# Hybrid decoder layer on one core: buffer sets of heads, inverses by rows over 128 partitions, later steps on transferred tiles, moved convolution pairs

## Chip, core and metric

The kernel runs on one NeuronCore of a Trainium2 chip (trn2). The time is the device time of one execution in microseconds (us), the median over runs; lower is better.

## What is computed

One layer with two groups of heads that run side by side, for 2048 tokens of width 1024, float32. One RMSNorm and one projection to 8208 columns feed both; a second projection brings 2048 columns back to 1024, a residual is added, and a last RMSNorm closes it.

```python
proj = rmsnorm(x, norm_in_w) @ w_in                        # 2048 x 1024 @ 1024 x 8208
qkv  = silu(causal_depthwise_conv(qkv, conv_qkv_w))        # 8 heads x 128, 4 taps
q, k = l2norm(q) * 128**-0.5, l2norm(k); beta = sigmoid(b_g)
g    = -exp(A_log) * softplus(a_g + dt_bias)               # decay of each head and token
# per head, chunk by chunk (WY form): A = strict(k beta k^T * decay), T = (I + A)^-1
u, w = T @ (v beta), T @ (k beta exp(g))
v_new = u - w S;  o = (q exp(g)) S + causal(q k^T * decay) v_new
S = S exp(g_last) + (k exp(g_last - g))^T v_new            # state 128 x 128, carried on
o   = rmsnorm(o, gdn_norm_w) * silu(z_g)
y_c = gate_b * (conv3(gate_c * h_c) + conv_b) * silu(z_c)  # 8 groups x 128 channels
out = rmsnorm(x + concat(o, y_c) @ w_out, final_norm_w)
```

## The kernel before

**Halves and pairs.** The tokens are done in two halves of 1024. In each half the projection is made as 32 *pairs* of 128 columns: `kq` (keys and queries of a head), `vz` (its values and output gate), `ca` and `cb` (the convolution group). `quad` makes a pair with seven products of 512 columns on TensorE (Strassen's form, float16 in two parts), 84 matmuls of 128x128 by 128x512 for each pair, from the tiles `xop` and the weights `g` (first half) or `gr` (second half, loaded from DRAM). The weights of the first half are loaded as `raw`, squared, scaled and split by ScalarE (ACT), VectorE (DVE) and GpSimd (POOL) while the first half runs; they are also written to DRAM (`wc`). Pair results stand in six tiles `t4` (`c1`, `c2`, `vacc`, ...), and a pair starts only when enough of them are free.

**Heads.** `gdn` runs for 16 heads (8 in each half; `idx` is the head's number over both). The steps: the convolved keys and queries go to two tiles `kq` (one for each block of 512 tokens); products of keys with keys and queries times the decay go to two tiles `NA`; the 32x32 blocks on the diagonal go by DMA to DRAM (`nd`) and back as `nb`, one block on each of 32 partitions; `invert` inverts them on POOL in place (60 TENSOR_TENSOR instructions); the inverse goes by DMA to DRAM (`wd`) and into `Wt`, when the head before has finished with it; DVE transposes to `Vt` and small matmuls (`Q`) put together the 128x128 inverse; then eight chunks of the recurrence follow (`ps_r`, `r`, `u`, `S_all`, with the output in the one PSUM bank `ps_o`). `gdn_post` copies the output from `ps_o` to `oc`, norms it, multiplies by the gate (`zb`, read back from DRAM) and stores it (`mixd`).

**Buffers.** `kq` and `NA` are rings of four tiles. The same rings serve before at the start (`x2`, the tokens of the first half) and in `later_x`, which prepares the second half's tokens in 16 steps (`x2` and `o16`), each step ending in a DMA to `x1d`. Head 0 begins after the first half's tokens; head 1's keys wait for the end of `later_x` (the mark `x1d`); each later head's keys wait for the recurrence of the head two before. The first thing that `gdn_post` of head 0 does is to wait for `x1d`.

**Order.** The instructions of each engine stand in one fixed order. A planner in the kernel (`Clock`, `do`) issues them while it follows its own estimate of each engine's time: a step is put into its engine's queue when the estimate says that its inputs are there, with a lead for each engine (`LEAD`; 0 for DVE), and `either` picks POOL or DVE for an addition. A number in `do(..., lead=-4.0)` puts the step that much later than its inputs. At run time an engine that waits for one instruction's input holds up all behind it.

Of the kernel before, what the change touches and what calls it, by code (L numbers as in the profile page):

```python
# [23 lines left out]
DRAIN, SEM = 0.2, 0.06  # L24
SAFE = -4.0
LEAD = {"PE": -0.4, "ACT": 0.0, "DVE": 0.0, "POOL": 0.0, "SP": -2.0}
# [200 lines left out]
def hybrid_layer_kernel(ctx, tc, x, norm_in_w, w_in, conv_qkv_w, A_log, dt_bias, gdn_norm_w,  # L227
# [65 lines left out]
    def mark(*key):  # L293
        done.add(key)
        marks[0] += 1
# [65 lines left out]
    def acq(kind):  # L361
        while not slots[kind]:
            yield None
        return bank(kind)
# [41 lines left out]
    for n in range(2 * CB):  # L406
        x2 = hd.tile([P, NC * P], F32, tag=("kq", "NA")[n // CB], name="x2", bufs=4)
        xt0.append(x2[:, 0:D])
# [17 lines left out]
    for half in range(2):  # L426
        convs = [(f, half, g) for g in range(G) for f in ("ca", "cb")]
        for i in range(H):
            pair("kq", half, i)
            if i == 0:  # L430
                plan.append(("gates", half, 0, None))
            n = ((4, 2, 2, 2, 2, 2, 1, 1), (2, 1, 2, 1, 2, 1, 2, 2))[half][i]
            for c in convs[:n]:
                pair(*c)
            convs = convs[n:]
            pair("vz", half, i)
        for c in convs:
            pair(*c)
# [152 lines left out]
    def first_x():  # L591
# [14 lines left out]
        def block0():  # L606
            for k in range(KD):
                pt = yield from acq("t")
                yield from trans(pt, k, 0)
                o = xop[X11 if k < KT else X21]  # L610
                yield from do(ACT.activation, kept(k), pt, AF.Copy, scale=sx_of(k))
                rel(pt)
                yield from split16(o[:, k % KT], kept(k))
                mark("x", X11 if k < KT else X21, k % KT)

        def block1():
            for i in range(CB, 2 * CB):
                yield from norm_tile(xt0[i], junk[:, i % 2])
            for kt in range(KT):
# [5 lines left out]
                yield from do(ACT.activation, f22, pt, AF.Copy, scale=sx_of(kt + KT))  # L625
                rel(pt)
                pt = yield from acq("t")
                yield from trans(pt, kt, 1)
# [20 lines left out]
    def later_x():  # L649
        yield from need(("x0",), ("rows",))  # L650
        xs = [hd.tile([P, NC * P], F32, tag="kq", name="x2", bufs=4) for _ in range(2)]
        ovs = []
        for _ in range(2):
            o16 = hd.tile([P, NC * P], F32, tag="NA", name="o16", bufs=4)
            ovs.append(o16.bitcast(F16)[:, 0:14 * QW].rearrange("p (o s w) -> p o s w", o=7, s=2))
# [364 lines left out]


    def taps(half, t, raw, accs, p, k, key):
        yield from need(key)
# [66 lines left out]
    def sumsq(acc, src):  # L1090
        junk = sm.tile([P, P], BF16, tag="junk", name="junk")
        yield from do(ACT.activation, junk, src, AF.Square, accum_out=acc)

    def gdn(half, h, st):
# [40 lines left out]
        for b in range(2):  # L1135
# [53 lines left out]
        for b in range(2):  # L1189
            yield from do(DVE.tensor_tensor, kqs[b][:, :, 1, :], qe[:, b * CB:(b + 1) * CB], kqs[b][:, :, 1, :],  # L1190
                          op=ALU.mult)

# [18 lines left out]
        for a, q0 in ((0, 0), (2, 0), (1, 32)):  # L1211
            r0 = a * 32
            yield from do(DVE.transpose, V[r0:r0 + 32, :, q0:q0 + 32], W[r0:r0 + 32, :, r0:r0 + 32])
        Q = hd.tile([P, NC, 64], F32, tag="Q", name="Q")
# [70 lines left out]
    def gdn_post(half, h, b, po, qss):  # L1285
        idx = half * H + h
        nq = CB * 4
        sl = slice(b * nq, (b + 1) * nq)
        if idx == 0:
            yield from need(("x1d",))  # L1290
        if idx or b:
# [9 lines left out]
        yield from do(DVE.transpose, on, osq)  # L1301
        op = sm.tile([P, nq], F32, tag="op", name="op")
# [12 lines left out]
        yield from do(DVE.tensor_tensor, ocv, ocv, osq, op=ALU.mult)  # L1315
        yield from do(DVE.scalar_tensor_tensor, zb, oc, gnw, zb, op0=ALU.mult, op1=ALU.mult)
        t0 = half * NC + b * CB
# [4 lines left out]
    def invert(nb, W, idx):  # L1322
        npart = 4 * NC
        tmp = hd.tile([npart, 16 * 16], F32, tag="nbt", name="nbt")
# [6 lines left out]
        yield from do(POOL.memset, nb.rearrange("p r x -> p (r x)")[:, 0:1024:33], -1.0)  # L1331
# [113 lines left out]
    def split_mix():  # L1445
        for t in range(NT):
# [13 lines left out]
            if t < 4:  # L1460
                yield from need(("rec", 2 * H - 2 + t // 2, 1))
            else:
                yield from need(("mixfree", t - 4))
            for h in range(2):
                m = hd.tile([P, 2, KM // 2 * P], F16, tag=("kq", "NA")[t % 2], name="mm", bufs=4)
                mr = mraw.pop((t, h))
# [156 lines left out]
```

## Time and profile before

| | |
|---|---|
| median of 3 runs | 2098.22 us (2096.51 to 2103.34) |
| profiled execution | 2094.53 us, span 2092.8 us |
| PE (TensorE) busy | 1914.5 us, 91% of the span |
| DVE busy | 1390.3 us, 66% |
| ACT busy | 960.5 us, 46% |
| POOL busy | 1003.3 us, 48% |
| TensorE clock granted | 0.967 of 2.4 GHz, mean |

The profile is one execution. An engine's busy time is the time in which at least one of its instructions runs; the matmuls' ends are modelled. Idle time of an engine matters only where others wait for it. All instructions that the planner issues carry one line number, so groups are read by their tiles: `NA<-ps_t,cj,E` writes `NA` from `ps_t`, `cj` and `E`.

### The profile page before, as it was taken

The page shows a single profiled execution, that of the slowest core. Times are in us where ns is not written, and L with a number is a line of the kernel's source. Part 1 is how long each engine was busy: PE and PEld are TensorE (multiplying, and loading weights), DVE is VectorE, ACT ScalarE, POOL GpSimd, SP SyncE. Part 2 cuts the span into 40 slices and gives each one's busy share as a digit, 9 for nine tenths or more (in the row PEclk, how much of TensorE's full clock was granted, in tenths as well). Part 3 has the DMA queues.
Part 4 walks back from the last instruction along what each step waited for, and adds up shares of the span by engine and source line. Part 5 has one row for each costly group of instructions (what it writes and reads, how often), then busy time and mean ns, then how long its engine had stood idle before and what let it go on. Part 6 is the DMA issues. An engine that isn't in the chain of part 4 may idle for free.

```text
span 2092.8 us, 29911 instructions
## 1 busy us (share of the span) xinstructions
PE 1914.5 (91%) x10832; PEld 1041.8 (50%) x10832; DVE 1390.3 (66%) x2547; ACT 960.5 (46%) x1879; POOL 1003.3 (48%) x1238
## 2 busy tenths in 40 slices
PE   3798996798888989888999999999999999999998
PEld 2343443345444545444566565565665664444443
DVE  5788777988686889895757667766766553532311
ACT  6565656555444555653545435344344232532300
POOL 3227521678383858597372774746755721100000
PEclk9899998899898999999999999999999999999999
DMA  5466676455776675447365456564344348433110
GB/s 148 101 175 155 175 184 165 111 135 143 96 148 107 150 151 155 126 131 292 124 187 160 126 191 195 192 189 145 119 130 125 103 134 312 151 99 113 61 51 30
DMA packets 231194, 302.66 MB, mean 145 GB/s; under 512 B 48381, under 2 KB 161414, under 8 KB 230150
## 3 DMA queue, kind: packets, MB, share of 16 engines
q1 hardware_dynamic: 231046, 300.75, 52.0%
q8 instruction: 85, 1.39, 0.3%
q14 instruction: 63, 0.52, 0.1%
HBM read 188.36 MB, written 112.33 MB: 144 GB/s over the span
## 4 chain that ended last, share of the span: by engine, by line
PE 53%; POOL 6%; DMA 4%; DVE 3%; issue 2%; ACT 1%; SPq 0%; DVEq 0%; POOLq 0%; ACTq 0%
PE ps_d L202 43%; PE ps_t L202 6%; POOL nb L202 3%; PE ps_r L202 3%; POOL nbt L202 2%; PE ps_o L202 2%; DMA raw<-in_w_in_dram 1%; DVE kq L202 1%; DVE g L202 1%; DMA wd<-nb 1%; DMA zb<-zd 1%; DMA wc<-g 1%; DVE c L202 0%; DMA mr<-mixd 0%; POOL raw L202 0%
## 5 line engine op out<-in xcount | busy, mean ns | idle before, releaser
L202 PE MATMUL ps_d<-xop,g 128*128 128x512 f16 x2688 | 659.4, 393 | 57.0 <-ACT c L202 26.0
L202 PE MATMUL ps_d<-xop,gr 128*128 128x512 f16 x2688 | 645.2, 379 | 2.6 <-DMA xop<-x1d 2.6
L202 PEld LDWEIGHTS <-g 128*128 128x128 f16 x2688 | 266.1, 101 | 349.1 <-issue 86.8
L202 PEld LDWEIGHTS <-gr 128*128 128x128 f16 x2688 | 261.2, 99 | 241.2 <-issue 3.2
L202 POOL TENSOR_TENSOR nbt<-nb 32x30 f32<-32x30 f32 (+14 forms) x480 | 317.8, 662 | 84.1 <-DMA nb<-nd 49.3
L202 POOL TENSOR_TENSOR nb<-nb,nbt 32x30 f32<-32x30 f32 (+14 forms) x480 | 331.5, 691 | 35.8
L202 ACT ACTIVATE c<-ps_d 128x512 f32<-128x512 f32 x320 | 189.5, 593 | 325.4 <-PE ps_d L202 306.3
L202 PE MATMUL ps_d<-wo,mm 128*128 128x512 f16 x1536 | 333.9, 380 | 4.0 <-ACT mm L202 3.6
L202 PEld LDWEIGHTS <-mm 128*128 128x128 f16 x1536 | 149.5, 98 | 186.7 <-ACT mm L202 5.5
L202 POOL TENSOR_TENSOR oss<-oss,nhalf_pow 128x16 f32<-128x16 f32 x32 | 99.6, 3114 | 155.1 <-DVE oss L202 155.1
L202 DVE SCALAR_TENSOR_TENSOR kq<-c,wq,kq 128x512 f32<-128x512 f32 x192 | 166.7, 872 | 4.6
L202 POOL TENSOR_TENSOR p<-p,nhalf_pow 128x2 f32<-128x2 f32 (+1 forms) x51 | 40.9, 801 | 199.3 <-DVE p L202 168.3
L202 DVE SCALAR_TENSOR_TENSOR res<-ps_d,msc,res 128x512 f32<-128x512 f32 x32 | 22.6, 746 | 168.9 <-PE ps_d L202 168.9
L202 POOL TENSOR_TENSOR c<-c,c 128x512 f32<-128x512 f32 (+1 forms) x33 | 57.3, 1738 | 159.8 <-ACT c L202 114.8
L202 DVE SCALAR_TENSOR_TENSOR g<-raw,wsc,g 128x1024 f16<-128x1024 f32 (+1 forms) x96 | 116.5, 1221 | 11.5 <-ACT g L202 11.2
L202 ACT ACTIVATE g<-raw,wsc 128x1024 f16<-128x1024 f32 (+1 forms) x96 | 95.8, 1001 | 59.4 <-PE ps_d L202 24.2
L202 POOL TENSOR_TENSOR stat<-stat,nhalf_pow 128x1 f32<-128x1 f32 x16 | 9.7, 604 | 234.0 <-DVE stat L202 234.0
L202 DVE TENSOR_TENSOR c<-ps_d,c 128x512 f32<-128x512 f32 x128 | 87.3, 682 | 42.5 <-PE ps_d L202 41.2
L202 ACT ACTIVATE mm<-mr,msc 128x1024 f16<-128x1024 f32 x32 | 36.0, 1145 | 158.5 <-PE ps_d L202 125.1
L202 ACT ACTIVATE u<-ps_r 128x128 f32<-128x128 f32 x128 | 35.2, 275 | 147.2 <-PE ps_r L202 144.5
L202 POOL TENSOR_TENSOR raw<-raw 128x512 f32<-128x512 f32 x31 | 41.8, 1349 | 119.6 <-DVE st L202 74.4
L202 DVE TENSOR_TENSOR c<-c,c 128x512 f32<-128x512 f32 (+1 forms) x63 | 58.3, 926 | 52.1 <-ACT c L202 49.8
(226 smaller groups left out, 2794.7 us busy)
## 6 DMA issues: line engine op xcount, KB each, us to landing
gr<-wc SPq DMA_DIRECT2D x96, 512.0 KB, 3.9
raw<-in_w_in_dram SPq DMA_DIRECT2D x64, 512.0 KB, 11.2
wc<-g SPq DMA_DIRECT2D x64, 512.0 KB, 9.1
wc<-g SPq DMA_DIRECT2D x96, 256.0 KB, 4.5
wor<-in_w_out_dram SPq DMA_DIRECT2D x32, 512.0 KB, 5.5
mr<-mixd SPq DMA_DIRECT2D x32, 512.0 KB, 5.0
x<-in_x_dram SPq DMA_DIRECT2D x16, 512.0 KB, 7.3
E<-gd SPq DMA_DIRECT2D x16, 512.0 KB, 5.9
```

The costliest lines, as they stand in the source:

```text
L202: return raw(*a, **k)
```

## The change

Five things. `kq` and `NA` become two sets of two tiles each: set 1 for even heads from head 2 on, set 0 for head 0 and the odd heads; `later_x` uses set 1. So head 1's keys wait for head 0's recurrence, block by block, and head 2's also for `x1d`. `gdn_post` of head 0 waits for `x1d` only after the copy out of `ps_o`. `invert` works on 128 partitions: each 32x32 block stands on four partitions (`nb`, loaded four times), and partition group *a* makes the rows of the inverse whose number leaves *a* when divided by 4, in `nbx` (8x32); it takes 62 TENSOR_TENSOR instructions and 5 MEMSETs, and four DMAs write the rows. Four DVE steps get a negative lead. `PLAN` changes how many convolution pairs stand behind each head; the sum in each half stays 16, and the last five of the second half now come after head 15's values, instead of three.

```diff
-SAFE = -4.0
+PLAN = ((3, 2, 2, 2, 2, 2, 2, 1), (2, 1, 2, 1, 2, 1, 2, 0))
+SAFE = -5.0
+LATE = -5.0
...
-            n = ((4, 2, 2, 2, 2, 2, 1, 1), (2, 1, 2, 1, 2, 1, 2, 2))[half][i]
+            n = PLAN[half][i]
... (block1 of the first tokens)
+                yield from need(("xk", kt), ("xk", kt + KT))
... (later_x: x2 in kq1, o16 in NA1, two buffers each)
+    def side(idx):
+        return "1" if idx and idx % 2 == 0 else "0"
... (conv_k)
-            if idx >= 2:
-                yield from need(("rec", idx - 2, b))
-            elif b == 0:
-                yield from need(("x0",) if h == 0 else ("x1d",))
+            if idx == 2:
+                yield from need(("x1d",))
+            if idx:
+                yield from need(("rec", max(idx - 2, 0), b))
+            else:
+                yield from need(("x0",))
-            st["kq"][b] = hd.tile([P, CB, 2, P], F32, tag="kq", name="kq", bufs=4)
+            st["kq"][b] = hd.tile([P, CB, 2, P], F32, tag="kq" + side(idx), name="kq", bufs=2)
... (gdn)
-            if half == 0 and h == 1:
-                yield from need(("x1d",))
-            NAs[b] = hd.tile([P, CB, 2, P], F32, tag="NA", name="NA", bufs=4)
+            NAs[b] = hd.tile([P, CB, 2, P], F32, tag="NA" + side(idx), name="NA", bufs=2)
-        nb = hd.tile([npart, 32, 32], F32, tag="nb", name="nb")
-        yield from do(SP.dma_start, nb.rearrange("p r x -> p (r x)"), nd.rearrange("a c r x -> (a c) (r x)"), lead=0.0)
+        nb = hd.tile([P, 32, 32], F32, tag="nb", name="nb")
+        for a in range(4):
+            yield from do(SP.dma_start, nb[a * npart:(a + 1) * npart].rearrange("p r x -> p (r x)"),
+                          nd.rearrange("a c r x -> (a c) (r x)"), lead=0.0)
... (kq<-qe,kq: lead=LATE; Vt<-Wt: lead=-3.0; in gdn_post on<-osq and zb<-oc: lead=LATE)
... (gdn_post)
-        if idx == 0:
-            yield from need(("x1d",))
         yield from do(ACT.activation, oc, pov, AF.Copy, back=9.0)
         rel(po)
+        if idx == 0:
+            yield from need(("x1d",))
... (invert)
-        for m in range(30, 0, -1):
-            n = 31 - m
-            tv = tmp[:, 0:m * n].rearrange("p (r x) -> p r x", x=n)
-            yield from do(POOL.tensor_tensor, tv, nb[:, 0:m, m:m + 1].to_broadcast([npart, m, n]),
-                          nb[:, m:m + 1, m + 1:32].to_broadcast([npart, m, n]), op=ALU.mult)
-            yield from do(POOL.tensor_tensor, nb[:, 0:m, m + 1:32], nb[:, 0:m, m + 1:32], tv, op=ALU.subtract)
+        for m in range(31):
+            n, nr = 31 - m, m // 4 + 1
+            tv = tmp[:, 0:nr * n].rearrange("p (r x) -> p r x", x=n)
+            yield from do(POOL.tensor_tensor, tv, X[:, 0:nr, m:m + 1].to_broadcast([P, nr, n]),
+                          nb[:, m:m + 1, m + 1:32].to_broadcast([P, nr, n]), op=ALU.mult)
+            yield from do(POOL.tensor_tensor, X[:, 0:nr, m + 1:32], X[:, 0:nr, m + 1:32], tv, op=ALU.subtract)
-        yield from do(SP.dma_start, wd.rearrange("a c r x -> (a c) (r x)"), nb.rearrange("p r x -> p (r x)"), lead=0.0)
+        for a in range(4):
+            yield from do(SP.dma_start, wd.rearrange("a c (r g) x -> g (a c) r x", g=4)[a],
+                          X[a * npart:(a + 1) * npart], lead=0.0)
```

On DVE, where head 1's keys are convolved (`kq<-c_1837` before, `kq<-c_1604` after; `o_630` and `o_631` are steps of `later_x`, `r` and `S_all` chunks of head 0's recurrence). Before:

```order
L202 TENSOR_SCALAR r<-vp 128x128
...
L202 COPY S_all<-ps_r 128x128
L202 TENSOR_TENSOR o_631<-xc,o_631 128x3x128
...
L202 SCALAR_TENSOR_TENSOR kq<-c_1837,wq,kq 128x4x128 x3
L202 SCALAR_TENSOR_TENSOR r<-ps_r,dec,vp 128x128
```

After:

```order
L204 SCALAR_TENSOR_TENSOR S_all<-S_all,dec,ps_r 128x128
...
L204 TENSOR_TENSOR o_630<-xa,o_630 128x4x128
L204 TENSOR_TENSOR xc<-xa,xc 128x128
L204 SCALAR_TENSOR_TENSOR kq<-c_1604,wq,kq 128x4x128
...
L204 SCALAR_TENSOR_TENSOR r<-ps_r,dec,vp 128x128
L204 SCALAR_TENSOR_TENSOR kq<-c_1604,wq,kq 128x4x128
```

Before, head 1's first key step stands behind the last step of `later_x`; after, it stands among these steps, between the chunks of head 0's second block.

On the DMA queue of SP, where the blocks of head 1 go out (`nd`) and come back (`nb`). Before:

```order
L202 DMA x1d<-o_631 128x7x256
L202 DMA nd<-NA 32x4x32 x4
L202 DMA wc_136<-g 128x2048
...
L202 DMA nd<-NA 32x4x32 x4
L202 DMA nb<-nd 32x1024
```

After:

```order
L204 DMA nd<-NA 32x4x32 x4
L204 DMA raw<-in_w_in_dram 128x8x128
L204 DMA nb<-nd 32x1024 x4
...
L204 DMA x1d<-o_630 128x7x256
L204 DMA wc_135<-g 128x1024 x2
L204 DMA wd<-nbx 256x1x32 x4
L204 DMA Wt_215<-wd 32x8x32 x3
...
L204 DMA x1d<-o_631 128x7x256
```

The `x1d` row before and the last `x1d` row after are the sixteenth and last of `later_x`. Head 1's blocks came back behind it; now the whole way of head 1 through DRAM stands ahead of it, the inverse written back included.

On POOL, the inverse of head 0. Before:

```order
L202 TENSOR_TENSOR nbt<-nb 32x30
L202 TENSOR_TENSOR nb<-nb,nbt 32x30
L202 TENSOR_TENSOR nbt<-nb 32x58
L202 TENSOR_TENSOR nb<-nb,nbt 32x29x2
L202 TENSOR_TENSOR nbt<-nb 32x84
```

After:

```order
L204 MEMSET nbx 128x256
L204 MEMSET nbx 32x8 x4
...
L204 TENSOR_TENSOR nbt<-nbx,nb 128x31
L204 TENSOR_TENSOR nbx<-nbx,nbt 128x31
L204 TENSOR_TENSOR nbt<-nbx,nb 128x30
```

The number of instructions stays nearly the same, on four times the partitions; the elements on each partition go from at most 240 to at most 76.

## Rows read from the trace of the kernel before

**Rows 1.** Stretches: us, engines' busy us (instructions), granted clock, DMA share, GB/s.

```profile
250.00:470.00 220.00, 181.59 (x872) 94.20 (x872) 173.87 (x318) 124.94 (x232) 89.23 (x93) 0.90 0.59 145
470.00:670.00 200.00, 166.96 (x1030) 94.81 (x1027) 148.43 (x265) 100.53 (x202) 123.16 (x149) 0.90 0.67 123
670.00:850.00 180.00, 167.97 (x953) 93.92 (x952) 150.11 (x256) 100.76 (x181) 132.32 (x149) 0.99 0.62 144
850.00:970.00 120.00, 106.09 (x701) 60.91 (x701) 101.53 (x182) 67.25 (x145) 82.30 (x96) 0.97 0.54 157
970.00:1090.00 120.00, 114.15 (x694) 67.89 (x693) 77.27 (x157) 49.71 (x110) 73.49 (x101) 1.00 0.59 201
1090.00:1740.00 650.00, 649.07 (x4104) 384.92 (x4103) 434.75 (x781) 272.87 (x580) 368.77 (x489) 1.00 0.49 153
```

**Rows 2.** The same stretches, instructions on `xop` alone: PE, DVE, ACT.

```profile
250.00:470.00 220.00, 157.64 (x656) 0.00 (x0) 0.00 (x0) 0.90 0.59 145
470.00:670.00 200.00, 128.50 (x495) 0.00 (x0) 0.00 (x0) 0.90 0.67 123
670.00:850.00 180.00, 143.89 (x606) 0.00 (x0) 0.00 (x0) 0.99 0.62 144
850.00:970.00 120.00, 80.54 (x327) 0.00 (x0) 0.00 (x0) 0.97 0.54 157
970.00:1090.00 120.00, 94.24 (x386) 0.00 (x0) 0.00 (x0) 1.00 0.59 201
1090.00:1740.00 650.00, 550.05 (x2302) 0.00 (x0) 0.00 (x0) 1.00 0.49 153
```

**Rows 3.** `later_x`, head 0's output copy, head 1's first key step (last: the timeline).

```profile
L202 SPq DMA_DIRECT2D x1d<-o x16: 370/371/4483, 94.9 to 351.8; - x16
L202 ACT ACTIVATE oc<-ps_o x32: 573/597/607, 351.7 to 1735.8; 128x512 f32<-128x512 f32 x32
...
351.86 2.33 DVE L202 SCALAR_TENSOR_TENSOR kq<-c,wq,kq 128x512 f32<-128x512 f32 x3
```

**Rows 4.** The chain that ended last, from 630 to 1090 us.

```profile
by line: PE ps_d L202 24.5%; POOL nb L202 11.9%; POOL nbt L202 10.7%; PE ps_t L202 8.6%; issue 4.8%; DMA raw<-in_w_in_dram 4.6%; DVE g L202 3.7%; DMA wd<-nb 3.4%; DVE kq L202 2.8%; DMA zb<-zd 2.6%; DMA wc<-g 2.5%; PE ps_r L202 2.5%; PE ps_o
633.33 15.76 DMA wd<-nb
```

**Rows 5.** POOL's inverse: two groups of the page, three of single forms.

```profile
L202 POOL TENSOR_TENSOR nbt<-nb 32x30 f32<-32x30 f32 (+14 forms) x480 | 317.8, 662 | 84.1 <-DMA nb<-nd 49.3
L202 POOL TENSOR_TENSOR nb<-nb,nbt 32x30 f32<-32x30 f32 (+14 forms) x480 | 331.5, 691 | 35.8
...
L202 POOL TENSOR_TENSOR nbt<-nb 32x30 f32<-32x30 f32 x32 | 12.0, 376 | 50.5 <-DMA nb<-nd 49.3
L202 POOL TENSOR_TENSOR nb<-nb,nbt 32x30 f32<-32x30 f32 x32 | 10.1, 315 | 2.5
L202 POOL TENSOR_TENSOR nbt<-nb 32x84 f32<-32x84 f32 x32 | 15.2, 474 | 2.5
```

**Rows 6.** DMAs: KB each, median us to landing; last, both transfers of `nb`.

```profile
E<-gd SPq DMA_DIRECT2D x16, 512.0 KB, 5.9
nd<-NA SPq DMA_DIRECT2D x128, 16.0 KB, 1.5
...
DMA to landing us min/median/max: 1.9/2.4/15.8
```

**Rows 7.** DVE's waits for transfers: total, times, longest.

```profile
DVE Vt L202 <- DMA Wt<-wd: 17.1, 6, 7.8
DVE kq L202 <- DMA qe<-gd: 6.8, 2, 4.7
```

**Rows 8.** One DVE form, without an inverse (250 to 390) and beside one (794 to 851).

```profile
L202 DVE SCALAR_TENSOR_TENSOR g<-raw,wsc,g 128x1024 f16<-128x1024 f32 x11 | 14.0, 1276 | 2.3 <-ACT g L202 2.3
L202 DVE SCALAR_TENSOR_TENSOR g<-raw,wsc,g 128x1024 f16<-128x1024 f32 x5 | 7.3, 1465 | 0.0
```

More of the change, by code (lines that the diff above doesn't have):

```diff
@@ L406, in hybrid_layer_kernel @@
     for n in range(2 * CB):
-        x2 = hd.tile([P, NC * P], F32, tag=("kq", "NA")[n // CB], name="x2", bufs=4)
+        x2 = hd.tile([P, NC * P], F32, tag=("kq", "NA")[n // CB] + str(n // 2 % 2), name="x2", bufs=2)
         xt0.append(x2[:, 0:D])
@@ L614, in block0 @@
                 mark("x", X11 if k < KT else X21, k % KT)
+                mark("xk", k)
         def block1():
@@ L650, in later_x @@
         yield from need(("x0",), ("rows",))
-        xs = [hd.tile([P, NC * P], F32, tag="kq", name="x2", bufs=4) for _ in range(2)]
+        xs = [hd.tile([P, NC * P], F32, tag="kq1", name="x2", bufs=2) for _ in range(2)]
         ovs = []
         for _ in range(2):
-            o16 = hd.tile([P, NC * P], F32, tag="NA", name="o16", bufs=4)
+            o16 = hd.tile([P, NC * P], F32, tag="NA1", name="o16", bufs=2)
             ovs.append(o16.bitcast(F16)[:, 0:14 * QW].rearrange("p (o s w) -> p o s w", o=7, s=2))
@@ L1090, in sumsq @@
     def sumsq(acc, src):
-        junk = sm.tile([P, P], BF16, tag="junk", name="junk")
-        yield from do(ACT.activation, junk, src, AF.Square, accum_out=acc)
+        yield from do(ACT.activation, junk_sq[:, 0:P], src, AF.Square, accum_out=acc)
     def gdn(half, h, st):
@@ L1190, in gdn @@
             yield from do(DVE.tensor_tensor, kqs[b][:, :, 1, :], qe[:, b * CB:(b + 1) * CB], kqs[b][:, :, 1, :],
-                          op=ALU.mult)
+                          op=ALU.mult, lead=LATE)
         if idx:
@@ L1212, in gdn @@
             r0 = a * 32
-            yield from do(DVE.transpose, V[r0:r0 + 32, :, q0:q0 + 32], W[r0:r0 + 32, :, r0:r0 + 32])
+            yield from do(DVE.transpose, V[r0:r0 + 32, :, q0:q0 + 32], W[r0:r0 + 32, :, r0:r0 + 32],
+                          lead=-3.0)
         Q = hd.tile([P, NC, 64], F32, tag="Q", name="Q")
@@ L1300, in gdn_post @@
         yield from do(ACT.activation, osq, ocv, AF.Square)
-        yield from do(DVE.transpose, on, osq)
+        yield from do(DVE.transpose, on, osq, lead=LATE)
         op = sm.tile([P, nq], F32, tag="op", name="op")
@@ L1315, in gdn_post @@
         yield from do(DVE.tensor_tensor, ocv, ocv, osq, op=ALU.mult)
-        yield from do(DVE.scalar_tensor_tensor, zb, oc, gnw, zb, op0=ALU.mult, op1=ALU.mult)
+        yield from do(DVE.scalar_tensor_tensor, zb, oc, gnw, zb, op0=ALU.mult, op1=ALU.mult, lead=LATE)
         t0 = half * NC + b * CB
@@ L1323, in invert @@
         npart = 4 * NC
-        tmp = hd.tile([npart, 16 * 16], F32, tag="nbt", name="nbt")
-        for m in range(30, 0, -1):
-            n = 31 - m
-            tv = tmp[:, 0:m * n].rearrange("p (r x) -> p r x", x=n)
-            yield from do(POOL.tensor_tensor, tv, nb[:, 0:m, m:m + 1].to_broadcast([npart, m, n]),
-                          nb[:, m:m + 1, m + 1:32].to_broadcast([npart, m, n]), op=ALU.mult)
-            yield from do(POOL.tensor_tensor, nb[:, 0:m, m + 1:32], nb[:, 0:m, m + 1:32], tv, op=ALU.subtract)
-        yield from do(POOL.memset, nb.rearrange("p r x -> p (r x)")[:, 0:1024:33], -1.0)
+        X = hd.tile([P, 8, 32], F32, tag="nbx", name="nbx")
+        Xf = X.rearrange("p r x -> p (r x)")
+        yield from do(POOL.memset, Xf, 0.0)
+        for a in range(4):
+            yield from do(POOL.memset, Xf[a * npart:(a + 1) * npart, a:256:36], -1.0)
+        tmp = hd.tile([P, 256], F32, tag="nbt", name="nbt")
+        for m in range(31):
[4 more added lines that the diff above has]
+            yield from do(POOL.tensor_tensor, X[:, 0:nr, m + 1:32], X[:, 0:nr, m + 1:32], tv, op=ALU.subtract)
         wd = dram.tile([4, NC, 32, 32], F32, tag="wd", name="wd", bufs=2)
-        yield from do(SP.dma_start, wd.rearrange("a c r x -> (a c) (r x)"), nb.rearrange("p r x -> p (r x)"), lead=0.0)
+        for a in range(4):
+            yield from do(SP.dma_start, wd.rearrange("a c (r g) x -> g (a c) r x", g=4)[a],
+                          X[a * npart:(a + 1) * npart], lead=0.0)
         if idx:
@@ L1460, in split_mix @@
             if t < 4:
-                yield from need(("rec", 2 * H - 2 + t // 2, 1))
+                yield from need(("rec", 2 * H - 2 + t // 2 % 2, 1))
             else:
@@ L1464, in split_mix @@
             for h in range(2):
-                m = hd.tile([P, 2, KM // 2 * P], F16, tag=("kq", "NA")[t % 2], name="mm", bufs=4)
+                m = hd.tile([P, 2, KM // 2 * P], F16, tag=("kq", "NA")[t % 2] + "10"[t // 2 % 2], name="mm", bufs=2)
                 mr = mraw.pop((t, h))
```

## The prediction

> **What bounds the kernel now.** I read the stretch table first, with the pace of the projection beside it, then the chain of waits, then the groups of POOL and DVE. In the table [rows 1] the reader is to see two regimes. From 1090 to 1740 us PE is busy 649.07 of 650 us at clock 1.00: nothing that shortens another engine's work, or moves a wait, gives time there. From 250 to 1090 us PE stands still for 38, 33, 12, 14 and 6 us (stretch less busy time), and until 670 its clock is 0.90 on average, so it ran at 1.2 GHz for a part of that stretch. The pace says the same [rows 2]: 84 matmuls on `xop` are one pair, so a pair takes 220 / (656 / 84) = 28.2 us, then 33.9, 25.0, 30.8 and 26.1 us, against 23.7 us from 1090 to 1740 (the 40 matmuls of the second half's gates are among the 386, which changes nothing here). The best long stretch before 970 is 25.0 us a pair, and it has whole inverses in it.
>
> Two things hold the early stretches back. First, head 1 waits for `later_x`: the last of its 16 transfers is issued at 351.8 us, head 0's first output block leaves `ps_o` at 351.7, and head 1's first key step runs at 351.86 [rows 3]. Until then head 1's pair keeps two of the six `t4` tiles, and new pairs wait for tiles. Second, from 630 to 1090 us POOL's inverse makes up 11.9 + 10.7 = 22.6% of the chain that ended last, 104 of 460 us [rows 4]. DVE is the next in line: 83.4% busy at 670 to 850 and 84.6% at 850 to 970, 77.5% (651.2 of 840 us) over 250 to 1090 [rows 1].
>
> **The change part by part**, against the profiled execution's own 2094.53 us (2092.8 span and 1.7 around it); the median of the runs shown is 3.7 us higher.
>
> *Head 1 earlier.* Head 1's keys now wait for head 0's recurrence, which no longer waits for `x1d` with its bank; in the order the key steps come among the steps of `later_x`, and head 1's blocks go to DRAM and back before its end. The stall that goes is that of 250 to 470 us: 7.81 pairs at 28.2 us; at 25.0 they take 195, so **-25 us**. Bounds: 0 if other waits keep the tiles, -35 at the 23.7 us of the late stretch. What is late next there is head 2, which still needs `x1d`; its pair is the tenth in the list, where head 1's was the seventh, so less stands idle meanwhile.
>
> *The inverse.* Before it costs (317.8 + 331.5) / 16 = 40.6 us of POOL for each head. Afterwards there are 62 instructions, on 31 sizes with 1560 elements a partition in all, 50 on average. The forms with 30 elements take 376 and 315 ns, that with 84 takes 474, so 1.8 ns an element [rows 5]: 376 and 315 plus 20 x 1.8 give 412 and 351 ns, 31 x 0.763 = 23.7 us. The five MEMSETs have no like in the rows; at the 315 ns of the cheapest form they add 1.6. Together 25.3, so -15 us a head. Bounds: 0 if an instruction costs the 676 ns mean of the 960 whatever its size (62 x 0.676 = 42), -28 if time goes by elements alone (40.6 x 1560 / 4960 = 12.8). I take the value by the size rows, since small forms stand in them.
>
> *Its transfers.* `nb` is now loaded four times, 512 KB in all: a 512 KB load (`E`) lands in 5.9 us, the one of 128 KB in 2.4 [rows 6], so +3.5. The inverse goes out in pieces of 128 bytes, 256 in each of four DMAs; `nd`, also in such pieces, 128 in each DMA, lands in 1.5 us, so about 3 for each of four side by side, and three more issues, +1.5 over the 2.4. Together +5 a head; from +1 (the four overlap fully) to +27 (both legs at the 15.8 of the row's worst case, less 2 x 2.4).
>
> On the path: the chain from 630 to 1090 spends 104 us in inverses, of which 15 / 40.6 go, -38, and the legs of heads 4 to 7 come back, +20; heads 2 and 3, before that chain, give 2 x (15 - 5) = -20. Together **-38 us**. Heads 8 to 15 give nothing, since PE covers them.
>
> *Steps put later.* DVE waits 17.1 us for `Wt` and 6.8 for `qe` [rows 7]. A later place lets other work go first; DVE is not always on the path, so I count half, **-12 us** (0 to -24). Behind the waiting transposes stand weight splits and pair sums, which ACT and PE wait for. The price is 3 us on `Vt` in each head's own way, which the landing takes anyway, and 5 us on steps of `gdn_post`, whose stores no one needs before the output projection.
>
> *DVE beside POOL.* The same DVE form takes 1276 ns where no inverse runs and 1465 beside head 5's [rows 8], 15% more. With 15 us less inverse for seven heads (105 us), DVE at about 83% busy and 15% of that, 13 us of DVE work go; half of it on the path, **-6 us** (0 to -13).
>
> *Moved pairs, the start, more issues.* The pairs of a half are the same in number, and at the end PE is busy 649 of 650 us, so their place costs nothing while the last head stays covered; if it does not, one wait of head 15 for PE is in sight, a few us. `xk` waits for what those steps read anyway: 0. Six more issues a head on SP, which mostly waits: 0.
>
> **Sum:** -25 - 38 - 12 - 6 = -81. Then DVE would carry 651.2 - 13 = 638 us in 840 - 81 = 759 us, 84%: as much as it does in its fullest stretches, and for 500 us on end. I do not expect every stretch to reach that, and take a fifth off: **-65 us**, 2029.5 for the profiled execution, **2033 us** for the median. What is late next is DVE.
>
> **One rule against it.** The row for `nd` shows 16 KB in pieces of 128 bytes landing in 1.5 us [rows 6]. The Trainium skill, page "DMA: Bandwidth & Descriptors", section "Specifications", wants transfers of 512 bytes and more for line rate and says that below this the DMA reads, modifies and writes. The change writes the inverse in just such pieces. By the row the leg costs +1.5 us; by the rule the write is slower by an amount that the page gives no time for here. The rival on transfers below holds it.
>
> **The rivals.**
>
> *DVE is the bound already* (0.20). For it: 77.5% on average with over 83% in two stretches [rows 1]. Against it: PE and ACT wait for heads, not for splits, where DVE is at 74% (470 to 670). If DVE can't go above 80.5% on average, the stretch takes 651.2 / 0.805 = 809 us, -31: **2067**.
>
> *PE becomes the bound* (0.08). If the stretch from 250 to 1090, 29.4 pairs (2470 / 84), went at 23.7 us, it would take 697 instead of 840, -143: **1955**. At 25.0 it is 735, -105. For it: the clock would stay at 1.00. Against it: the first half alone carries the weight splits, and DVE would be over 90% busy.
>
> *The transfers eat the inverse's gain: slower* (0.10). One mechanism: a head now waits for the last of four loads and the last of four writes, in a queue full of weight traffic (DMA share 0.54 to 0.67 [rows 1]). The chain has one `wd` of 15.76 us [rows 4], the median being 2.4 [rows 6]. If both legs come to that, a head pays +27 - 15 = +12; for heads 2 to 7, +72, less the 25 of head 1 and some of the waits: +30, **2128**. It decides from 15 us for both legs together: there the inverse's gain is used up.
>
> *It doesn't do what it says* (0.07). There is one bank `ps_o` and one `oc`. Head 0's second block still keeps the bank until its first has been through `gdn_post`, which needs `x1d`; if head 1 then waits with its recurrence as long as it did with its keys, the first term is gone, and with DVE full the rest is about -8: **2090**.
>
> **How the numbers follow.** The forecast has 0.55, by itself 2000 to 2060. Measurements of this kernel can't tell less than 0.3%, about 6 us. Faster by more: 0.55 + 0.20 + 0.08 and a third of the last, 0.85; within: 0.05; slower: 0.10. The range of 8 in 10 leaves out the slower rival and most of the one with PE as the bound, and takes in DVE as the bound and the inverse's bounds: 1985 to 2088.
>
> **What would show it.** Head 1's first key step near 300 us instead of 352; POOL's inverse groups at about 25 us a head; first-half pairs at 25 to 27 us from 250 on, with PE's clock nearer 1.00; the stretch in which PE is full beginning 60 us earlier and lasting as long as before; DVE no longer waiting for `Wt` and `qe`. It is wrong if the inverse's instructions keep 0.6 us at 50 elements, if `nb` and `wd` land later than 8 us together above before, if head 1's first key step stays near 352 us, or if PE idles in the second half.

## The result, and the profile after

The changed kernel takes 2079.84 us (median of 4 runs, 2075.96 to 2081.78) against 2097.36 for the kernel before: a ratio of 0.9909, interval 0.9884 to 0.9934. That is 17.5 us faster, where 65 were forecast; 2080 lies in the range, but far from 2033. The profiled execution took 2081.03 us, with a span of 2079.3.

First the table of stretches of the changed kernel, for which before has [rows 1]; the columns are those of before.

```profile
250.00:470.00 220.00, 191.30 (x977) 104.99 (x975) 174.33 (x339) 131.90 (x251) 107.05 (x171) 0.89 0.59 152
470.00:670.00 200.00, 173.51 (x1020) 99.06 (x1021) 152.37 (x284) 107.64 (x207) 100.40 (x165) 0.91 0.70 142
670.00:850.00 180.00, 161.89 (x982) 93.47 (x980) 143.76 (x276) 101.99 (x199) 83.91 (x118) 0.93 0.62 140
850.00:970.00 120.00, 107.78 (x618) 61.27 (x616) 81.21 (x154) 56.66 (x108) 56.76 (x93) 0.96 0.59 191
970.00:1090.00 120.00, 119.31 (x777) 68.17 (x776) 76.31 (x160) 57.67 (x125) 53.20 (x111) 1.00 0.58 183
1090.00:1740.00 650.00, 640.62 (x3988) 379.42 (x3987) 414.27 (x776) 270.33 (x565) 258.58 (x512) 1.00 0.51 162
```

The same stretches with the instructions on `xop` alone, as in [rows 2].

```profile
250.00:470.00 220.00, 155.29 (x640) 0.00 (x0) 0.00 (x0) 0.89 0.59 152
470.00:670.00 200.00, 139.84 (x569) 0.00 (x0) 0.00 (x0) 0.91 0.70 142
670.00:850.00 180.00, 131.41 (x538) 0.00 (x0) 0.00 (x0) 0.93 0.62 140
850.00:970.00 120.00, 88.76 (x366) 0.00 (x0) 0.00 (x0) 0.96 0.59 191
970.00:1090.00 120.00, 99.93 (x424) 0.00 (x0) 0.00 (x0) 1.00 0.58 183
```

By 850 us the projection has not gained at all: 640 + 569 + 538 = 1747 matmuls since 250, where before had 656 + 495 + 606 = 1757 [rows 2]. From 250 to 1090 there are 2532 against 2468 (the rows below, before first). The 64 more are 64 / 84 of a pair, at 23.7 us a pair 18 us: the whole gain. It comes after 850 us (790 against 713). PE is busy 754 of 840 us in place of 737, but still stands still for 29, 26, 18 and 12 us in the first four stretches; its clock is lower at 670 to 850 (0.93, before 0.99), and DVE is busy 628 us, less than before's 651.

```profile
250.00:1090.00 840.00, 604.82 (x2468) 0.00 (x0) 0.00 (x0) 0.94 0.61 149
```

```profile
250.00:1090.00 840.00, 615.23 (x2532) 0.00 (x0) 0.00 (x0) 0.93 0.62 157
```

What the change does locally came almost to the number. First the inverse's two groups on its page [rows 5].

```profile
L204 POOL TENSOR_TENSOR nbt<-nbx,nb 128x60 f32<-128x60 f32 (+24 forms) x496 | 200.8, 405 | 121.3 <-DMA nb<-nd 84.7
L204 POOL TENSOR_TENSOR nbx<-nbx,nbt 128x60 f32<-128x60 f32 (+24 forms) x496 | 203.1, 409 | 38.1
```

The transfers of `later_x` (first and last issue), and in the next fence the timeline at head 1's first key step [rows 3].

```profile
L204 SPq DMA_DIRECT2D x1d<-o x16: 360/390/2199, 95.1 to 384.5; - x16
```

```profile
271.94 0.74 DVE L204 SCALAR_TENSOR_TENSOR kq<-c,wq,kq 128x512 f32<-128x512 f32 x1
```

The inverse's transfers: KB each, median us from issue to landing [rows 6].

```profile
nb<-nd SPq DMA_DIRECT2D x64, 128.0 KB, 2.7
wd<-nbx SPq DMA_DIRECT2D x64, 32.0 KB, 2.0
```

An inverse takes (200.8 + 203.1) / 16 = 25.2 us (forecast 25.3 with its five memsets, which come to 0.7), head 1's keys begin at 272 us in place of 352, and the 17 us that DVE waited for `Wt` [rows 7] are 3.8. The transfers cost a head about 4 us in the median, where 5 were forecast, since it waits for the last of four: from the first issue of `nb` to the inverse's first instruction 4.9 us (before 2.6), and in heads 8 to 15 from the first issue of `wd` to the first load of `Wt` 4.0 (before 2.5). So each edit does locally what was said, and the time is not there.

### The profile page after: what moved, and what is told of

It is laid out like the page before. It is cut to its first block, busy times and chain, and to the rows that moved or that the text cites. A ratio compares the mean times of both kernels' runs of the same rounds, so it can differ in the third digit from the quotient of the medians.

```text
span 2079.3 us, 30141 instructions
## 1 busy us (share of the span) xinstructions
PE 1918.4 (92%) x10832; PEld 1051.1 (51%) x10832; DVE 1325.5 (64%) x2559; ACT 964.2 (46%) x1871; POOL 765.9 (37%) x1330
## 4 chain that ended last, share of the span: by engine, by line
PE 52%; DVE 3%; issue 1%; ACT 1%; DMA 1%; POOL 0%; SPq 0%; DVEq 0%; POOLq 0%; ACTq 0%
PE ps_d L204 43%; PE ps_t L204 5%; PE ps_r L204 3%; PE ps_o L204 2%; DVE kq L204 0%; DVE wo L204 0%; POOL oss L204 0%; DMA mr<-mixd 0%; DMA gr<-wc 0%; DVE c L204 0%; DVE ab L204 0%; ACT c L204 0%; DVE NA L204 0%; DVE vacc L204 0%; ACT junk_sq L204 0%
## 5 line engine op out<-in xcount | busy, mean ns | idle before, releaser
L204 POOL TENSOR_TENSOR nbt<-nbx,nb 128x60 f32<-128x60 f32 (+24 forms) x496 | 200.8, 405 | 121.3 <-DMA nb<-nd 84.7
L204 POOL TENSOR_TENSOR nbx<-nbx,nbt 128x60 f32<-128x60 f32 (+24 forms) x496 | 203.1, 409 | 38.1
L204 DVE SCALAR_TENSOR_TENSOR kq<-c,wq,kq 128x512 f32<-128x512 f32 x192 | 155.4, 812 | 4.3 <-ACT kq L204 0.3
L204 DVE SCALAR_TENSOR_TENSOR g<-raw,wsc,g 128x1024 f16<-128x1024 f32 (+1 forms) x96 | 108.2, 1134 | 27.1 <-ACT g L204 26.3
L204 POOL TENSOR_TENSOR c<-c,c 128x512 f32<-128x512 f32 (+1 forms) x31 | 52.3, 1689 | 155.4 <-ACT c L204 100.4
## 6 DMA issues: line engine op xcount, KB each, us to landing
raw<-in_w_in_dram SPq DMA_DIRECT2D x64, 512.0 KB, 11.1
```

Source lines behind the costliest of these rows:

```text
L204: return raw(*a, **k)
```

## The experiments

Differences are medians against runs of the kernel before that were taken together with each (the changed kernel: -17.5). "In its order" means that the planner counts the original step, so that every engine's other instructions stand where they stood, and only what is issued differs. The first theories: **S**, the prediction's sum; **T**, waits for tiles alone set the pace; **O**, each new order of the planner has its own luck.

**e1**, in before's order, and **e2**, in the order of after: the inverse gone, and the inverse longer.

```diff
-            yield from do(POOL.tensor_tensor, tv, ...)
+            yield from do(GHOST.tensor_tensor, tv, ...)   # e1, both steps: counted, not issued
+            nc.gpsimd.tensor_tensor(tv, ...)              # e2: the product a second time, not counted
```

> The kernel before with its order of instructions kept on every engine, but the 60 subtractions and products of each inverse are not issued (the inverse is left out, so the blocks of W are not the reference's): POOL does 40 us less a head, everything else stands where it stood. Theory S (the prediction's: the inverse lies on the path with its share of the chain): at least the 104 us of the chain from 630 to 1090 less what is late next, so 50 to 100 us faster. Theory O (the order: a shorter inverse pays as long as the order is kept, and the planner's new order gave it back): the same gain here, 50 to 100. Theory T (the tiles: pairs wait for t4 tiles that the recurrence frees, and PE's fixed place for the recurrence sets that, the inverse lies beside it): less than 15 us.

> The changed kernel with its order kept, but the product of each of the 31 steps of an inverse is issued twice (same values), so an inverse takes about 38 us of POOL in place of 25 and nothing else moves. Theory S and theory O: 12.6 of 15 us of the term of 38 come back, 25 to 35 us slower than the changed kernel. Theory T: within 10 us of the changed kernel (2080).

e1: 2051.16 us, **-46** (ratio 0.9775, 0.9762 to 0.9788). e2: 2250.59, 1.0732 (1.0716 to 1.0748) of before, **171 us more than the changed kernel**. None of the theories expected the pair. Taking 40.6 us from every head gives 46 us in all; adding 12.6 us to every head (202 us of POOL) costs 171. Theory T falls, and so do S and O in e1, if narrowly: in this order even the whole inverse is worth less than half of its 104 us in the chain [rows 4].

What e1 can give is held down by the order that it keeps. Head 8's blocks are fetched back at 1014 us, POOL's last step of the inverse is now done at 1016, and the write-back is still issued at 1055, since it stands in SP's queue behind transfers that wait for other work. From `nb` to `wd` that is 41.3 us, where before takes 42.5.

```profile
1013.79 0.31 SPq L202 DMA_DIRECT2D nb<-nd  x1
1055.12 0.37 SPq L202 DMA_DIRECT2D wd<-nb  x1
```

So the 46 us are what leaving the inverse out gives while its readers keep their places, not a bound for a new order.

Why a longer step costs so much is seen in the waits of ACT and PE (total us, times, longest): first e2's, then the changed kernel's.

```profile
ACT E L204 <- POOL E L204: 83.2, 10, 15.5
PE ps_d L204 <- ACT c L204: 63.3, 12, 10.0
```

```profile
ACT E L204 <- POOL E L204: 20.6, 8, 4.8
PE ps_d L204 <- ACT c L204: 4.2, 5, 2.0
```

One such place in e2's timeline (start us, us, in brackets the idle time before): POOL, ACT and PE near 1640 us.

```profile
1638.34 0.21 POOL L204 TENSOR_TENSOR nbx<-nbx,nbt 128x8 f32<-128x8 f32 x1
1638.50 2.90 POOL L204 TENSOR_TENSOR oss<-oss,nhalf_pow 128x16 f32<-128x16 f32 x1
1641.36 1.10 POOL L204 TENSOR_SCALAR_AFFINE_SELECT E<-E 128x1024 f32<-128x1024 f32 x1
...
1642.49 0.69 ACT L204 ACTIVATE E<-E,ngc 128x128 f32<-128x128 f32 x2 [15.13 <-POOL E L204]
...
1645.03 0.58 ACT L204 ACTIVATE c<-ps_d 128x512 f32<-128x512 f32 x1
...
1645.65 1.86 PE L204 MATMUL ps_d<-xop,gr 128*128 128x512 f16 x4 [9.87 <-ACT c L204]
```

The mask of the next head's `E` stands behind the inverse and a step of `gdn_post` (`oss`) in POOL's queue, ACT stands 15 us at the exponential of `E`, behind that in ACT's queue are the copies `c<-ps_d`, and PE waits 10 us for one of them, in the second half, where nothing of the inverse was thought to be on the path. The order is cut to measure: what comes late is paid on three engines, what comes early finds its readers in their old places.

**e3** and **e4**, the kernel before with one part alone, planned anew: the new inverse and its transfers, or the two buffer sets with head 1 in head 0's. **e5** has both, with before's leads and places of pairs.

```diff
-            elif b == 0:
-                yield from need(("x0",) if h == 0 else ("x1d",))      # e4, e5
+            if idx:
+                yield from need(("rec", max(idx - 2, 0), b))
...
-        for m in range(30, 0, -1):                                    # e3, e5
+        for m in range(31):
```

> The kernel before with one part of the change alone: the inverse by rows on 128 partitions with its four loads and four stores (and the squares of a head written to the large junk tile, which makes room for it). The planner puts the order anew. Theory S: -38 us. Theory O: less than half of that, -15 to +10, with the recurrences of heads 3 to 5 stretched in PE's order. Theory T: within 10 us of before.

> The kernel before with one part of the change alone: the two buffer sets, with head 1 in head 0's and no wait for the later x tiles. The planner puts the order anew. Theory S: -25 us, from the pairs between 250 and 470. Theories O and T: the stall moves to the next pair that finds no tile (head 2, or head 1's wait for head 0's recurrence), -10 to +10.

> The kernel before with two parts of the change, the buffer sets with head 1 in head 0's and the new inverse, but with the old places of the conv pairs and the old leads of the steps. Theory P (parts add up): e3 gave -13.6 and e4 -0.5, so about -14 against before, 2083, and the rest of the change, steps later and pairs moved, is worth the last 4 us. Theory O (each new order has its own luck, larger than the parts): off that sum by 10 us or more, in either direction; below 2070 would say that the moved pairs and later leads cost time.

e3: 2083.75, **-13.6** (0.9929, 0.9912 to 0.9946). e4: 2096.83, **-0.5** (0.9992, 0.9983 to 1.0). e5: 2058.48, **-36** (0.9827, 0.9803 to 0.9852). Alone each does what O said (T only e4); together they give 22 us more than the sum of theory P, and below 2070, as O had it. In e4 head 1's inverse runs from 363 to 426 us, though head 0's recurrence has ended at 328: the wait for `x1d` is gone, and the old inverse is what is late. And e5 is 18 us faster than the whole change (-36 against -17.5), so in these orders the rest of the change costs time.

**e6**, **e7**, **e8**, **e12**: one constant of the planner, how far it fills another engine's queue.

```diff
-BACK = 1.2
+BACK = 1.25    # e6: before, e7: after, e12: e5; e8: after with 1.1
```

> The kernel before, with nothing changed but one constant of the planner, BACK 1.25 us in place of 1.2 (how far ahead of PE's clock it fills another engine's queue): the same instructions in a somewhat other order. Theory P: within 6 us of before. Theory O: 8 to 25 us off, more likely slower, since before's constants are those that its author kept.

> The changed kernel with BACK 1.25 us in place of 1.2, else the same instructions. Theory P: within 6 us of the changed kernel (2080). Theory O: 8 to 30 us off, in either direction.

> The changed kernel with BACK 1.1 us in place of 1.2, else the same instructions. Theory P: within 6 us of the changed kernel (2080). Theory O: 8 to 30 us off, and the spread between this and the run with 1.25 is 15 us or more.

> The kernel of e5 (2058) with BACK 1.25 us in place of 1.2, else the same instructions. Theory O (luck of the order): 8 to 25 us slower, as in the kernel before (+26 for the same step) and the changed one (+25); then the three kernels keep their distances at 1.25, with this one 25 to 45 us below the kernel before at 1.25 (2120). If it stays within 6 us of 2058, the order of e5 is no lucky one.

e6: 2120.09, **+26** (1.0114, 1.009 to 1.0138). e7: 2105.44, **+11** (1.0052, 1.0034 to 1.0069), 29 above the changed kernel. e8: 2073.93, **-20** (0.9897, 0.9881 to 0.9913), 3 below it. e12: 2061.75, **-34.5** (0.9828, 0.9797 to 0.986), 1.5 from e5. O is right in e7 and, at the edge of its 25 us, in e6; in e8 it has the spread against e7 (31 us) and not the distance from the changed kernel; in e12 it is wrong. A constant that changes no work can move the kernels before and after by more than the change did, while e5 keeps its time in both orders that were tried. At 1.25 it is some 60 us below before (-34.5 against +26), but 26 of these are before's own loss.

**e9**, **e10**, **e11**: what the rest of the change costs. e9 is the changed kernel with the old places of the pairs; e10 is e5 with the later leads, e11 is e5 with the moved pairs. M: the moved pair costs; L: the later leads cost; P: the prediction, neither costs.

```diff
-            n = PLAN[half][i]                                                     # e9; e11 the reverse
+            n = ((4, 2, 2, 2, 2, 2, 1, 1), (2, 1, 2, 1, 2, 1, 2, 2))[half][i]
...
-            yield from do(DVE.transpose, V[r0:r0 + 32, ...], W[r0:r0 + 32, ...])   # e10
+            yield from do(DVE.transpose, V[r0:r0 + 32, ...], W[r0:r0 + 32, ...], lead=-3.0)
```

> The changed kernel with the conv pairs back in their old places (4, 2, 2, 2, 2, 2, 1, 1 in the first half in place of 3, 2, 2, 2, 2, 2, 2, 1; the second half's back too). Theory M (the moved pair costs: with three conv pairs before head 0's value pair, head 1's key pair comes one pair earlier, keeps two tiles until head 0's recurrence ends, and PE stands 24 us at the pair after it): that gap is gone, no wait of over 10 us for tiles between 250 and 300, and the run is 8 to 20 us faster than the changed kernel, 2060 to 2072. Theory L (the later leads are what costs): within 6 us of the changed kernel. Theory P (the prediction: moved pairs cost nothing): the same.

> The kernel of e5 (2058) with the later places of the five kinds of steps added: the products with qe, the transposes of Wt, the transpose and the last product of gdn_post. Theory P (the prediction's term): 5 to 12 us faster, 2046 to 2053. Theory L: 10 to 22 us slower, 2068 to 2080. Theory M: within 6 us.

> The kernel of e5 (2058) with the conv pairs in the changed kernel's places and nothing else. Theory M: 10 to 20 us slower, 2068 to 2078, with a gap of over 15 us between the projection's matmuls near 270 us. Theories L and P: within 6 us.

e9: 2073.31, **-23** (0.9882, 0.9856 to 0.9908). e10: 2067.71, **-28.5** (0.9854, 0.9823 to 0.9885). e11: 2078.36, **-18** (0.9906, 0.9877 to 0.9934). Theory L has the sign in e10 and P has not, though L's 10 us are not reached. So from e5's -36: later leads +7.5, the squares' lead (`SAFE`) +5.5, moved pairs +5.5 on top of these or +18 alone. Theory M's 18 are there without the leads; with them it is short of its bound. Steps of 5 us are within the luck of an order, so the causes have to be sought in the trace, and three things are seen there. The first: the stretch from 264 to 290 us, the changed kernel's row first, then e11's, then e5's.

```profile
264.00:290.00 26.00, 15.09 (x59) 11.31 (x58) 23.75 (x48) 15.52 (x38) 3.07 (x2) 0.58 0.54 146
```

```profile
264.00:290.00 26.00, 16.91 (x78) 12.65 (x77) 22.49 (x51) 14.07 (x28) 7.22 (x5) 0.69 0.40 113
```

```profile
264.00:290.00 26.00, 24.08 (x130) 14.48 (x131) 24.42 (x52) 18.39 (x39) 5.30 (x5) 1.00 0.50 130
```

With three conv pairs ahead, head 1's key pair is the sixth in the list and keeps two tiles until its second block is convolved; that block waits for head 0's recurrence, whose last product runs at 294 us, and its last key step ends at 311. The next value pair needs three of the other four tiles and begins at 288.5, PE has only the recurrence's short products to run, between which it waits for DVE and ACT, and the clock granted in the stretch is 0.58. With four pairs ahead (e5) PE is busy 24 of 26 us at clock 1.00. In e9 this gap is gone, but one of 15 us stands at 292: it moves rather than goes.

The second: the last load of a block of `Wt` (issues from, to) and the transposes into `Vt` that read it (first and last start), head 3 after, then head 3 before.

```profile
L204 SPq DMA_DIRECT2D Wt<-wd x4: 337/442/450, 576.1 to 577.5; - x4
L204 DVE STREAM_TRANSPOSE Vt<-Wt x3: 426/434/435, 592.1 to 594.3; 32x256 f32<-32x256 f32 x3
```

```profile
L202 SPq DMA_DIRECT2D Wt<-wd x4: 331/448/450, 649.1 to 650.5; - x4
L202 DVE STREAM_TRANSPOSE Vt<-Wt x3: 433/435/435, 650.8 to 652.3; 32x256 f32<-32x256 f32 x3
```

From the last issue to the first transpose heads 2 to 7 take on average 11.8 us after, 3.2 before, 5.5 in e5 and 10.6 in e10. The leads alone (e10 against e5) make 5.1 us. Over these six heads 8.6 us more than before are 52 us on the heads' own way (load, transposes, block products, recurrence), for 17.1 us that DVE was rid of [rows 7].

The third: the one bank `ps_o` and the one `oc`. An output block is copied out of `ps_o` when the last product of `gdn_post` on the block before (`zb<-oc`) has freed `oc`, and the second half of a recurrence needs the bank. That product is one of the steps put later. Head 5 in the changed kernel: the last product of its first block into `ps_o`, the product of head 4's last block, the copy, and the first product of head 5's second block.

```profile
845.86 0.39 PE L204 MATMUL ps_o<-NA,u 128*128 128x128 f32 x2
870.41 0.74 DVE L204 SCALAR_TENSOR_TENSOR zb<-oc,cols_b,zb 128x512 f32<-128x512 f32 x1
872.64 0.59 ACT L204 ACTIVATE oc<-ps_o 128x512 f32<-128x512 f32 x1
876.06 0.38 PE L204 MATMUL ps_r<-r,Wt 128*128 128x128 f32 x2
```

The same head in e5, the product of the block before first.

```profile
836.50 0.75 DVE L202 SCALAR_TENSOR_TENSOR zb<-oc,cols_b,zb 128x512 f32<-128x512 f32 x1
850.61 0.64 PE L202 MATMUL ps_o<-NA,u 128*128 128x128 f32 x2
851.28 0.60 ACT L202 ACTIVATE oc<-ps_o 128x512 f32<-128x512 f32 x1 [3.38 <-PE ps_o L202]
```

From a first block's last product to its copy heads 1 to 7 together wait 109 us in the changed kernel, 43 before, 12 in e5 and 65 in e10, which adds the leads alone. The recurrences of heads 3 to 5 take 75 us each after, 47 to 58 before, 49 to 54 in e5; and in heads 2 to 6 the one tile `Wt` is loaded no more than 2.7 us after the recurrence of the head before has ended with it (before: 15 us or more). What this costs in time no run shows by itself: e18 below has 67 us of such waits and is the fastest kernel that leaves nothing out.

**e13**, **e14**, **e15**, **e17**: what is late next, all in the changed kernel's order. D: DVE; R: the weights' loads; I: the rest of the inverse; F: the order itself.

```diff
-                yield from do(DVE.scalar_tensor_tensor, acc, x[j], ...)
+                yield from do(CUT.scalar_tensor_tensor, acc, x[j], ...)   # e13: counted in full, issued on 64 columns
...
-                yield from do(SP.dma_start, raw, src)
+                yield from do(load_flat, raw, src)                        # e14: same bytes, 4 KB pieces
...
-            yield from do(POOL.tensor_tensor, tv, ...)
+            yield from do(GHOST.tensor_tensor, tv, ...)                   # e15: as in e1; e17: all three
```

> The changed kernel with its order kept, but DVE's multiply-adds of the short convolutions (keys, queries, values and the conv pairs) work on 64 columns in place of 512 or 1024 (so the convolutions are not the reference's): some 10 us a head and 4 us a conv pair less of DVE, over 100 us less from 250 to 1090. Theory D (the prediction's: what is late next is DVE): 40 us or more faster than the changed kernel, 2040 or less. Theory F (the order itself: PE stands where it has been given only a recurrence's steps, whose chain of short steps no engine's length sets): less than 15 us.

> The changed kernel with its order kept, but each weight tile raw is loaded from 512 KB in one piece, 4 KB for each partition, in place of eight pieces of 512 bytes (so the weights are others): the same bytes in an eighth of the packets. Theory R (the weights' loads are late): 15 us or more faster, with the squares' wait for raw gone. Theories D and F: within 6 us of the changed kernel.

> The changed kernel with its order kept, but the 62 products and subtractions of each inverse are not issued (the inverse is left out): what e1 did in the order of before. Theory I (the inverse is still on the path): 30 us or more faster, as its lengthening cost 170. Theory F: 10 to 20 us, less than e1's 46, since less of it is left and its readers keep their places; a step that comes early gives little where one that comes late costs in full.

> The changed kernel with its order kept and the reductions of e13, e14 and e15 together (convolutions on 64 columns, weights' loads in one piece, inverse not issued; none of the three gives the reference's values). Alone they gave -40, -24 and -22 us. Theory A (three separate stretches of the path, one after the other): the sum, -86, 1994. Theory F (they lie beside each other, and the order's own waits stay under all three): -45 to -65, 2015 to 2035, with the gaps of some 13 us at pairs 15 and 27 still there. If one of them is the bound and the others cover: no more than -45.

e13: 2039.98, **-58** (0.9721, 0.9706 to 0.9735), 40.5 below the changed kernel. e14: 2056.31, **-42** (0.98, 0.9784 to 0.9817), 24 below. e15: 2058.46, **-39.5** (0.9807, 0.9788 to 0.9826), 22 below. e17: 1997.41, **-101** (0.9521, 0.9506 to 0.9537), 83 below, where the three alone make 86.5. So D is met at its bound, R with room (24 where 15 were asked, and ACT's 15.8 us of waiting for `raw` are gone), I and F are both missed, and A holds: the three add up. That is how it would be if the path passed from one engine to the next in short turns, with stretches of its own for each and none covering another. DVE is the largest of the three, not the bound. These are the rows from 250 to 1090 us of the changed kernel, of e13 and of e17.

```profile
250.00:1090.00 840.00, 753.79 (x4368) 426.97 (x4367) 627.98 (x1211) 455.86 (x886) 401.31 (x654) 0.93 0.62 157
```

```profile
250.00:1090.00 840.00, 777.77 (x4558) 446.05 (x4557) 544.09 (x1267) 468.68 (x926) 365.47 (x672) 0.94 0.64 163
```

```profile
250.00:1090.00 840.00, 806.10 (x4752) 463.74 (x4751) 561.32 (x1320) 483.90 (x960) 193.03 (x168) 0.96 0.52 169
```

84 us less of DVE in this stretch, in which more pairs were done, gave 40. Even in e17 PE stands still for 34 us; the order's own gaps, some 13 us near pair 27, stay as they were, and so do most of the waits for `ps_o` (88 of 109 us).

**e16** and **e18**: head 1's pair moved the other way, and once more with `BACK` at 1.15.

```diff
-            n = ((4, 2, 2, 2, 2, 2, 1, 1), ...
+            n = ((5, 2, 2, 2, 2, 2, 1, 0), ...
```

> The kernel of e5 (2058) with five conv pairs ahead of head 0's value pair in place of four (5, 2, 2, 2, 2, 2, 1, 0 in the first half), so head 1's key pair comes one pair later. Theory M (what counts is how long head 1's pair keeps two tiles before head 0's recurrence ends): the 9 us that PE stands near pair 9 go, 2045 to 2056. Theory P: within 6 us of 2058.

> The kernel of e16 (2051, head 1 and the new inverse, five conv pairs first, old leads) with BACK 1.15 us in place of 1.2: the best version that the runs point to, and a second order of it. If the gain of e16 is its own and not one order's luck: within 10 us of 2051, and 30 us or more below the changed kernel's 2080. Theory O (luck): 2065 or more.

e16: 2051.00, **-47** (0.9769, 0.9746 to 0.9791). e18: 2049.41, **-49** (0.9759, 0.9733 to 0.9785). M holds (some 10 us below e5, and the gap near pair 9 is gone), and a second order gives the same time. Neither leaves anything out, and both beat both kernels.

## Why the prediction was wrong

*The inverse on the path, -38.* This step failed: "the chain from 630 to 1090 spends 104 us in inverses, of which 15 / 40.6 go". The length was right (25.2 us), and the transfers nearly (about +4 a head, +5 forecast); the share of a chain is not a price. With no inverse at all e1 gives 46 us in before's order, in proportion 17 for 15 / 40.6 of it; the new inverse alone, in an order of its own, measured -13.6. Close behind the inverse the trace of before has a second chain, which the prediction named (one `ps_o`, one `oc`) and did not price here: from 558 to 1026 us each copy out of `ps_o` comes 1.7 to 12.9 us after the product of `gdn_post` that frees `oc` has begun, and the recurrences of heads 3 to 6 begin 1.9 to 9.3 us after such a copy. No run shortens that chain by itself, so its share in the miss stays open.

*Head 1 earlier, -25.* Its keys came at 272 us as said, and alone it gave -0.5 (e4), where its own old inverse is late. In the changed kernel its inverse is put together at 405.6 us, and its recurrence starts at 422, behind head 0's second output block.

```profile
405.05 0.59 ACT L204 ACTIVATE Wt<-ps_t 64x512 f32<-64x512 f32 x1 [3.99 <-PE ps_t L204]
418.14 0.74 DVE L204 SCALAR_TENSOR_TENSOR zb<-oc,cols_b,zb 128x512 f32<-128x512 f32 x1
420.54 0.57 ACT L204 ACTIVATE oc<-ps_o 128x512 f32<-128x512 f32 x1
422.18 0.49 PE L204 MATMUL ps_r<-r,Wt 128*128 128x128 f32 x2 [1.16 <-DVE r L204]
```

That block is copied 126 us after its last product (294.0), since head 0's first block goes through `gdn_post` only from 374 to 419, where the order holds it for `x1d`. With the new inverse head 1 pays: both together -36, where -63 was forecast. Part of this is the luck of before's order, which at `BACK` 1.25 loses 26 us while e5 loses 1.5; how much, four orders can't say.

*Steps put later, -12.* Wrong in sign: +7.5 (e10). That is one order each, and within the luck of an order. The working booked DVE's shorter wait as gain, the later transposes as a delay "which the landing takes anyway", and the steps of `gdn_post` as ones "whose stores no one needs". The trace of e10 has 5.1 us more than e5 between load and transposes in each head (10.6 - 5.5), and the stores may be late, but the last product also frees `oc`, and with it the bank that the next half of a recurrence needs: 65 us of such waits in e10, 12 in e5.

*Moved pairs, 0.* Wrong: +5.5 to +18. The text looked only at the end, where PE is full (now 640.62 of 650 us), not at the start, where one pair earlier for head 1 means two tiles kept for longer. Of the 9 us that PE stands still at the end, 6.2 are one wait for `mm`, when the second projection begins.

*DVE beside POOL, -6.* DVE's work from 250 to 1090 fell by 23 us where 13 were forecast. At e13's rate (40.5 for 84) that would be worth about 11, an estimate from these two.

*What is late next is DVE.* Half right: it is the largest of three, and its share of busy time (75% after, 77.5% before) never showed a limit.

*The rivals.* The transfers (2128) fall: both legs add some 4 us a head, far from the 15 at which this rival decides. Each 32 KB of `wd` in pieces of 128 bytes land in 2.0 us, where 128 KB landed in 3.3 before. The Trainium skill's page "DMA: Bandwidth & Descriptors", section "Specifications", wants at least 512 bytes for line rate; no run writes the new inverse in larger pieces, so what the small pieces cost here is not shown, beyond that the leg stays small. The gate that moves (2090) comes nearest in time, and its gate is in the trace: head 1's recurrence waits for `ps_o`, yet it starts 60 us earlier than before (422 and 483), so the first term was not gone for that reason alone. DVE as the bound (2067) is as near, with the wrong reason: it fell below its old share. None of the rivals held two edits that cost time and an order that is put anew.

Not settled: which step's luck makes up e6 and e7, and what each part is worth apart from its order. The steps of 5 to 8 us (`SAFE`, the leads, the pairs) and even the -13.6 of e3 stand on one order each, and a step of `BACK` alone moved two kernels by 26 and 29 us. Firmer is the pair of the first two terms: in four orders (e5, e12, and with the first pairs moved e16, e18) they gave 34.5 to 49 us, never 63.

## What to carry to other kernels

The share of an engine in the chain of waits bounds a gain only from above; what can be had goes up to the next path behind it. Leaving the work out with the order kept measures the gain in that order, where readers keep their places; a new order has to be measured anew. In this program, whose order is written out ahead, a step that came late was paid nearly in full (171 of 202 us) and one that came early hardly at all (46 of 650 before, 22 of 404 in the changed kernel's order), so ask of each moved or delayed step who reads it next on a head's own way, and who waits for the buffer that it frees. Before a change of 1% is believed or blamed, move a constant that changes no work and see how far the time moves by itself.

## What was not expected of the hardware

The same 512 KB of a weight tile land in 11.1 us in pieces of 512 bytes and in 5.1 us in pieces of 4 KB (e14), with the DMA engines' busy share from 250 to 1090 us at 0.62 and 0.49 for about the same GB/s (157 and 161). The rows are the changed kernel's and e14's: least, median and longest us to landing.

```profile
DMA to landing us min/median/max: 7.8/11.1/24.9
```

```profile
DMA to landing us min/median/max: 3.6/5.1/8.7
```
